# Reordering the steps of a compressed attention branch in a one-core decoder layer

## Chip, cores and metric

The kernel runs on one core of one Trainium2 chip. The metric is the device time of one execution in microseconds (us), as the median of three runs. The engines are named PE (TensorE, matrix multiply; PEld is its weight load), DVE (VectorE), ACT (ScalarE), POOL (GpSimd) and SP (SyncE, which here only issues the transfers).

## What is computed

One layer of a decoder on a sequence of 512 tokens with 1024 channels, in float32:

```python
h = rms_norm(x, attn_norm_w)
z = h @ w_in                      # pool input, q, k/v of three branches, gates
y_pool = pool_mixer(u_pool, pool_w, pool_scale) @ w_pool_br
y_attn = nsa_attention(q, k, v, nsa_g, ...) @ w_attn_br
x = x + (merge_g0 * y_pool + merge_g1 * y_attn) @ w_o
h = rms_norm(x, ffn_norm_w)
x = x + conv_ffn(h, w_up, conv_w, conv_b, w_down)
```

The attention has 16 heads of 64 channels in two groups of keys and values, and three branches whose outputs are added with sigmoid gates. Two of them see the 512 causal tokens (with 8 blocks out of 8 selected and a window of 512 both are plain causal attention, on keys and values of their own). The third one, the compressed branch, makes from the keys and from the values 31 blocks of 32 tokens each (stride 16), sends each block through a small network (`gelu(flat @ w1 + b1) @ w2`), and attends to those 31 keys.

## The kernel before

Every matrix product is done as three float32r products: each operand is split into a high part (a rounded copy, mostly on ACT, line 97) and a low part (the difference, on DVE or POOL, line 100), and `mm3` (lines 109 to 111) multiplies high by high, high by low and low by high. Weights come through a ring: `ring` (line 152) issues a transfer on SP into one of two `st` buffers and splits it into `hi` and `lo` tiles, of which there are six each. The kernel is written in a framework in which a program traces its instructions in order, and a scheduler then gives each engine a queue. It may move an instruction ahead of others on the same engine when those are not ready in its own estimate; on the chip every engine then works its queue in that order. Tiles of one tag in a pool share a fixed number of buffers. PSUM has eight banks: tag "g" (2 banks: `bank_g`), "s" (3, `bank_s`), "t" (2, `bank_t`) and "o" (1, `bank_o`).

The work before the attention stands as a list of calls (lines 529 to 553), and its order there is the priority that the scheduler sees:

- `kv_group(b)` and `q_group(gq)` (lines 338 and 357): a projection of 256 columns for four blocks of 128 tokens (`tg` in "s", 24 matmuls each), then norm and rope (`head_norm_rope`, line 285: on ACT x_, its square and a root; on DVE `hss`, two products and sum `h`, the reciprocal `hrs`, and `kd` or `qd`; a product on POOL), then transposes (`kt`, `qt` in "t") and the split into `KHL` or, for the queries, `qp` (lines 376 and 377, of tag "qo" with eight buffers).
- `pool_in`, `pool_mix`, `pool_out` (lines 392, 411, 424): the pooling mixer. `pool_mix` multiplies four groups (`pl` in "g") and splits them into `plo` (lines 102 and 103, tag "qo", too); `pool_out(c)` multiplies all four `plo` by a slice of `w_pbr` (`pb` in "g", two tiles, 24 matmuls).
- `cmp_in(i)` (line 440; i=0 keys, i=1 values): doubles the compressed branch's tokens on POOL (`dup`), transposes them (`ct`, two tiles in "t") and splits them into `X` (one buffer for both i), eight splits on ACT and DVE.
- `cmp_hid(i)` (line 459): two transfers of `cw1`, eight splits on ACT and POOL, 32 matmuls of 256 columns (`hp` in "g"), then `hs` (one instruction on ACT, two on DVE, lines 476 to 478), a transpose (`ht` in "g") and `cx`.
- `cmp_out(i)` (line 486): gelu by way of a tanh, the small product `kp` (in "o") and the split into `Kc` (keys) or `Vc` (values).
- `f_g0(c)` (line 525): a gate tile, 24 matmuls of 512 columns (`fm` in "g"), `zg` on DVE, tanh on ACT, `yp` on DVE.

The attention loop (lines 752 to 770) runs over 32 units u (head u // 2, branch u % 2) and one more turn. `scores(u)` (line 667) does for each block i of 128 queries the product `ss` in "s" (lines 691 and 692) and the softmax steps (lines 680 and 681); for i=0 both branches at once. `values(u)` (line 709) turns the probabilities (`tp`) and multiplies by the values (`op`). Between them lie `slot`s, at which PE gets pieces of gate tiles as filling (`fill`, line 590: `fm`, three matmuls a piece, kept behind the last `ss` by `issue_after`); the first two units get more of them (`START`, line 71: two pieces behind each `ss` of unit 0, one of unit 1). Weights for the filling are split ahead (`fetch`, line 579, the low part on POOL). The compressed branch is done for four heads at a time by `Cmp` (line 609): `score` (8 matmuls `sc`, then `cst` on DVE, line 624), `soft` (4 transposes `scq`, line 629, then the softmax, whose last step is `ce` on POOL, line 642) and `turn` (4 transposes `pct`, line 648, and `pc`), which `values` of the odd units reads (line 733). With `ORD = 0` and `DEPTH = 1` all three steps of the first four heads stand in turn u = 0: `score` and `soft` ahead of `scores(0)`, `turn` behind it.

Of the kernel before, what the change touches and what calls it, by code (L numbers as in the profile page):

```python
# [51 lines left out]
DEPTH = 1  # L52
# [6 lines left out]
ORD = 0  # L59
# [17 lines left out]
def layer(ctx: ExitStack, tc: tile.TileContext, par, masks, xT, w_kva, w_tm, w_fm, w_pl, w_pbr,  # L77
# [5 lines left out]
    def nm(s):  # L83
        cnt[0] += 1
        return f"{s}{cnt[0]}"
# [4 lines left out]
    def r32(ap):  # L90
        return ap.bitcast(F32)

    def split(hi, lo, src, scale=None, eng=None, cast=None):

        if scale is None:
            if cast is None:
                a.activation(hi, src, AF.Copy)  # L97
            else:
                cast.tensor_copy(hi, src)
            (eng or v).tensor_tensor(lo, src, r32(hi), ALU.subtract)  # L100
        else:
            a.activation(hi, src, AF.Copy, scale=scale)
            v.scalar_tensor_tensor(lo, src, scale, r32(hi), ALU.mult, ALU.subtract)
# [68 lines left out]
    def pv(n):  # L172
        o, w = _OFF[n]
        return pk[:, o:o + w] if o < NKEEP else pl_[:, o - NKEEP:o - NKEEP + w]
# [138 lines left out]
    def tok_gemm(ws, n):  # L313

        for t in range(NB):
            ps = bank_s("tg")
            tt = slice(t * P, (t + 1) * P)
            for k, (H, L) in enumerate(ws):
                pe.matmul(ps[:, :n], hh[k][:, tt], H, start=k == 0, stop=False)  # L319
                pe.matmul(ps[:, :n], hl[k][:, tt], H, start=False, stop=False)  # L320
                pe.matmul(ps[:, :n], hh[k][:, tt], L, start=False, stop=k == KC - 1)  # L321
            yield t, ps

    def tm_weights(i):
        return ring(w_tm[:, i, :1024], 256, 4, TW[i] and g) + ring(w_tm[:, i, 1024:], 256, 4, TW[i] and g)
# [12 lines left out]
    def kv_group(b):  # L338
        for t, ps in tok_gemm(tm_weights(b), 256):
            vin = heads(ps[:, 128:256])  # L340
            vh = V2[b][t][:, :, 0:DH]
            a.activation(vh, vin, AF.Copy, scale=rstd[:, t:t + 1])
            v.scalar_tensor_tensor(V2[b][t][:, :, DH:P], vin, rstd[:, t:t + 1], r32(vh), ALU.mult, ALU.subtract)

            k2 = pp.tile([P, 2, 2, DH], F32, tag="kq", name=nm("kd"), bufs=KQ)
            head_norm_rope(heads(ps[:, 0:128]), 2, t, 2 + b,
                           (k2, lambda x: x.unsqueeze(2).to_broadcast([P, 2, 2, DH])))
            tp = bank_t("kt")
            for G in range(2):
                pe.transpose(tp[:, G * P:(G + 1) * P], k2[:, G].rearrange("p a d -> p (a d)"), ident)  # L350
            tt = slice(t * P, (t + 1) * P)
            split(KHL[:, b, 0, :, tt], KHL[:, b, 1, :, tt], tp[:, :2 * P].rearrange("p (G q) -> p G q", q=P))
# [4 lines left out]
    def q_group(gq):  # L357
        qp = [qo.tile([P, 2, S], F32R, tag="qo", name=nm("qp"), bufs=8) for _ in range(2)]
        QP[2 * gq:2 * gq + 2] = qp
        for t, ps in tok_gemm(tm_weights(2 + gq), 256):  # L360


            q2 = pp.tile([P, 2, 2, DH], F32, tag="kq", name=nm("qd"), bufs=KQ)
            head_norm_rope(heads(ps[:, :256]), 4, t, 0,
                           (q2.rearrange("p b a d -> p a b d"),
                            lambda x: x.rearrange("p (a b) d -> p a b d", b=2)))
            if t % 2 == 0:
                tp = bank_t("qt").rearrange("p (b q) -> p b q", b=2)
            o = t % 2 * P
            for b in range(2):  # L370
                pe.transpose(tp[:, b, o:o + P], q2[:, b].rearrange("p a d -> p (a d)"), ident)
            if t % 2:
                tt = slice((t - 1) * P, (t + 1) * P)
                for a_ in range(2):
                    rh, rl = slice(64 * a_, 64 * a_ + 64), slice(64 - 64 * a_, 128 - 64 * a_)
                    a.activation(qp[a_][rh, :, tt], tp[rh], AF.Copy)
                    v.tensor_tensor(qp[a_][rl, :, tt], tp[rh], r32(qp[a_][rh, :, tt]), ALU.subtract)
# [46 lines left out]
    def pool_out(c):  # L424
        ws = ring(w_pbr[c], P, 8, POW[c] and g)
        for j in range(2):
            ps = bank_g("pb")
            mm3(ps, [(ws[2 * k + j], (plh[k], pll[k])) for k in range(4)])
            yp = ypp.tile([P, S], F32, tag=f"yp{2 * c + j}", name=f"yp{2 * c + j}")
            a.activation(yp, ps, AF.Copy, scale=0.5)  # L430
            ypool[2 * c + j] = yp
# [8 lines left out]
    def cmp_in(i):  # L440
        XX = p1.tile([P, 16, 2, 2, 32], F32R, tag="X", name=nm("X"))
        Xs[i] = XX
        X = (XX[:, :, 0], XX[:, :, 1])
        g.memset(r32(XX[:, :, :, 1, 31:32]), 0.0)
        split(X[0][:, :, 0, 31], X[1][:, :, 0, 31], pv("pos")[:, 16 * i:16 * i + 16])
        for G in range(2):
            tp = bank_t("ct")
            for t in range(NB):
                dup = p1.tile([P, 2, DH], F32, tag="dup", name=nm("dup"), bufs=3)
                g.tensor_copy(dup, kcd[i][t][:, G].unsqueeze(1).to_broadcast([P, 2, DH]))  # L450
                pe.transpose(tp[:, t * P:(t + 1) * P], dup.rearrange("p a d -> p (a d)"), ident)
            for lo_ in (0, 64):
                rr = slice(lo_, lo_ + 64)
                for c in range(2):

                    src = tp[rr].rearrange("p (n f b) -> p f n b", f=8, b=2)[:, :, c:c + 31, lo_ // 64]
                    split(X[0][rr, 8 * c:8 * c + 8, G, :31], X[1][rr, 8 * c:8 * c + 8, G, :31], src)

    def cmp_hid(i):
        X = Xs[i]  # L460
        hp = bank_g("hp")
        hv = hp[:, :256].rearrange("p (j h) -> p j h", j=2)
        for c in range(2):
            st = wr.tile([P, 1024], F32, tag="st", name=nm("st"), bufs=ring.bufs[0])
            nc.sync.dma_start(st, cw1[i, :, c * 1024:(c + 1) * 1024])
            for p_ in range(4):
                tag = ("hi", "lo")[p_ % 2]
                w = wr.tile([P, 2, 2, P], F32R, tag=tag, name=nm(tag), bufs=ring.bufs[1])
                split(w[:, 0], w[:, 1], st[:, 256 * p_:256 * p_ + 256].rearrange("p (b h) -> p b h", b=2),
                      eng=CW and g)  # L470
                for b in range(2):
                    q_ = 8 * c + 2 * p_ + b
                    pe.matmul(hv, X[:, q_].rearrange("p j g n -> p (j g n)"), w[:, :, b],
                              start=q_ == 0, stop=q_ == 15)
        hs = pp.tile([64, P], F32, tag="hs", name=nm("hs"))
        a.activation(hs, hp[:64, :P], AF.Copy)
        v.tensor_tensor(hs, hp[:64, P:256], hs, ALU.add)
        v.tensor_tensor(hs, hp[64:128, :P], hs, ALU.add)
        ht = bank_g("ht")
        pe.transpose(ht[:, :64], hs, ident[:64, :64])  # L480
        bias = pp.tile([P, 1], F32, tag="cb", name=nm("cb"))
        v.tensor_tensor(bias, ht[:, 31:32], b1[:, i:i + 1], ALU.add)
        cx[i] = pp.tile([P, 64], F32, name=f"cx{i}")
        v.tensor_scalar(cx[i], ht[:, :64], bias, None, ALU.add)
# [45 lines left out]
    for gi in range(4):  # L530
        pool_in(gi)
    kv_group(1)
    cmp_in(0)
    q_group(0)
    pool_mix()
    q_group(1)
    cmp_hid(0)
    cmp_in(1)
    pool_out(0)
    pool_out(1)  # L540
    q_group(2)
    pool_out(2)
    pool_out(3)
    cmp_hid(1)
    pre.close()
    q_group(3)
    mid = ExitStack()
    mp = pool(mid, "mp", side="right")
    for c in range(NPRE):
        f_g0(c, fm_tile(ring(w_fm[4 + c], P, KC), hh, hl), mp)  # L550
    cmp_out(0)
    cmp_out(1)
    mid.close()


# [193 lines left out]
    pcs = [Cmp(4 * q_) for q_ in range(4)]  # L749
    fetch(0)  # L750
    pbs = [None] * NU
    for u in range(NU + DEPTH):
        if u == ORD:
            pcs[0].score()
            pcs[0].soft()
        if u < NU:
            pbs[u] = scores(u)
        if u == max(ORD, DEPTH - 1):
            pcs[0].turn()
        w = u - DEPTH  # L760
        if w >= 0:
            values(w, pbs[w], pcs[w // 8])
            nq = w // 8 + 1
            if nq < 4:
                if w % 8 == 4:
                    pcs[nq].score()
                elif w % 8 == 5:
                    pcs[nq].soft()
                elif w % 8 == 7:
                    pcs[nq].turn()  # L770
# [195 lines left out]
```

## Time and profile before

| what | value |
|---|---|
| median of three runs | 843.49 us (843.36 to 844.0) |
| the profiled execution, its time | 842.97 us |
| its span, first to last instruction | 840.9 us |
| busy: PE, PEld | 817.7, 696.8 us |
| busy: DVE, ACT, POOL | 571.4, 464.4, 233.7 us |
| mean granted clock of PE | 0.994 |

All durations come from the one profiled execution. Times within it are us from the span's start. A busy PE means that matmuls are in flight. An engine's idle time matters only where it delays the end; here the chain that ended last goes through PE for 85% of the span. The granted clock is a share of full speed: 1.00 is 2.4 GHz, and 0.50 is the lower level of 1.2 GHz.

### The profile page before, as it was taken

Reading aid. Unit: us, or ns where it says so; the run is one execution under the profiler, and the core shown is the slowest. Engines: PE = TensorE matmul, PEld = TensorE weight load, DVE = VectorE, ACT = ScalarE, POOL = GpSimd, SP = SyncE. Lnnn points to the kernel's source line nnn. Section 1 sums busy time; section 2 is a strip of 40 time slices with the busy share of each in tenths; the row PEclk is TensorE's granted clock in tenths of the full one; section 3 lists DMA queues with packets and bytes.
Section 4 is the critical chain, followed back from the end, with each engine's and each line's share of the span. In section 5 each row is a group of like instructions: output and inputs, shape, how many; then the busy total and the mean of one; then the engine's idle time right before and its main releaser. Section 6 shows DMA issues by size and latency. Waiting matters only on the chain.

```text
span 840.9 us, 12107 instructions
## 1 busy us (share of the span) xinstructions
PE 817.7 (97%) x4291; PEld 696.8 (83%) x4291; DVE 571.4 (68%) x1194; ACT 464.4 (55%) x985; POOL 233.7 (28%) x326
## 2 busy tenths in 40 slices
PE   7999989989999999999999999999999999999998
PEld 6888878968878878788888888888888888888888
DVE  7599976778887888886565438877777777522321
ACT  6755767757787877785334436544554454322220
POOL 5696714347575655642001200000000000000000
PEclk9999989999999999999999999999999999999999
DMA  6333132330100101011443332233332333343430
GB/s 217 103 101 113 51 101 96 107 101 25 51 26 26 51 17 35 27 39 42 135 149 112 101 103 77 101 101 101 100 91 90 97 100 116 92 128 103 113 101 26
DMA packets 23116, 72.82 MB, mean 87 GB/s; under 512 B 2832, under 2 KB 3472, under 8 KB 23056
## 3 DMA queue, kind: packets, MB, share of 16 engines
q1 hardware_dynamic: 23056, 72.05, 27.5%
q8 instruction: 34, 0.56, 0.3%
q14 instruction: 26, 0.21, 0.1%
HBM read 69.94 MB, written 2.10 MB: 86 GB/s over the span
## 4 chain that ended last, share of the span: by engine, by line
PE 85%; DVE 7%; ACT 3%; DMA 2%; issue 1%; POOL 0%; SPq 0%; ACTq 0%; DVEq 0%; POOLq 0%
PE fm L109 16%; PE fm L111 16%; PE fm L110 16%; PE op L729 5%; PE dn L109 5%; PE dn L111 5%; PE dn L110 5%; PE tp L722 4%; PE ss L691 2%; PE ss L692 2%; PE tg L321 2%; PE tg L319 2%; PE tg L320 2%; DMA st<-in_w_fm 1%; PE pb L109 1%
## 5 line engine op out<-in xcount | busy, mean ns | idle before, releaser
L97 ACT ACTIVATE hi<-st 128x512 fp32r<-128x512 f32 (+3 forms) x253 | 152.2, 607 | 189.3 <-PE fm L110 89.6
L100 DVE TENSOR_TENSOR lo<-st,hi 128x512 fp32r<-128x512 f32 (+1 forms) x210 | 145.2, 695 | 100.5 <-ACT hi L97 99.2
L109 PE MATMUL fm<-h2h,hi 128*128 128x512 f32 x344 | 134.0, 389 | 0.0
L110 PE MATMUL fm<-h2l,hi 128*128 128x512 f32 x344 | 133.8, 389 | 0.0
L111 PE MATMUL fm<-h2h,lo 128*128 128x512 f32 x344 | 133.7, 389 | 0.0
L703 POOL TENSOR_TENSOR pb<-pb,sm 128x128 f32<-128x128 f32 (+3 forms) x128 | 91.8, 748 | 49.8 <-DVE sm L700 26.1
L681 ACT ACTIVATE pb<-pb,nm 128x384 f32<-128x384 f32 (+3 forms) x128 | 70.9, 555 | 16.2 <-DVE nm L680 15.4
L111 PEld LDWEIGHTS fm<-h2h,lo 128*128 128x128 f32 x344 | 64.6, 188 | 13.5
L110 PEld LDWEIGHTS fm<-h2l,hi 128*128 128x128 f32 x344 | 64.6, 188 | 13.4
L109 PEld LDWEIGHTS fm<-h2h,hi 128*128 128x128 f32 x344 | 64.6, 188 | 13.2
L109 PE MATMUL fm<-hh,hi 128*128 128x512 f32 x160 | 71.7, 448 | 0.0
L680 DVE CUSTOM_DVE_ANT_0 pb<-ss,mk 128x384 f32<-128x384 f32 (+3 forms) x128 | 58.9, 486 | 16.7 <-PE ss L692 13.2
L110 PE MATMUL dn<-gl,hi 128*128 128x512 f32 (+1 forms) x189 | 69.1, 365 | 0.0
L111 PE MATMUL dn<-gh,lo 128*128 128x512 f32 (+1 forms) x189 | 69.1, 365 | 0.0
L109 PE MATMUL dn<-gh,hi 128*128 128x512 f32 (+1 forms) x189 | 69.1, 365 | 0.0
L111 PE MATMUL fm<-hh,lo 128*128 128x512 f32 x160 | 63.4, 397 | 0.7 <-POOL lo L100 0.7
L100 DVE TENSOR_TENSOR ptl<-tp,pth 128x512 fp32r<-128x512 f32 (+1 forms) x96 | 56.6, 594 | 10.8 <-ACT pth L97 10.2
L110 PE MATMUL fm<-hl,hi 128*128 128x512 f32 x160 | 63.4, 396 | 0.0
L97 ACT ACTIVATE pth<-tp 128x512 fp32r<-128x512 f32 (+1 forms) x96 | 49.3, 517 | 22.8 <-PE tp L722 22.5
L100 POOL TENSOR_TENSOR lo<-st,hi 128x512 fp32r<-128x512 f32 x36 | 47.2, 1313 | 41.6 <-ACT hi L97 35.6
L319 PE MATMUL tg<-hi,hh 128*128 128x256 f32 x192 | 54.4, 286 | 0.0
L320 PE MATMUL tg<-hi,hl 128*128 128x256 f32 x192 | 54.4, 286 | 0.0
(256 smaller groups left out, 1815.9 us busy)
## 6 DMA issues: line engine op xcount, KB each, us to landing
st<-in_w_up SPq DMA_DIRECT2D x43, 512.0 KB, 3.5
st<-in_w_dn SPq DMA_DIRECT2D x24, 448.0 KB, 3.4
st<-in_w_fm SPq DMA_DIRECT2D x20, 512.0 KB, 3.5
st<-in_w_tm SPq DMA_DIRECT2D x12, 512.0 KB, 3.4
st<-in_w_ab SPq DMA_DIRECT2D x8, 512.0 KB, 3.5
st<-in_w_o SPq DMA_DIRECT2D x8, 512.0 KB, 3.4
x<-in_xT SPq DMA_DIRECT2D x15, 256.0 KB, 3.7
st<-in_cw SPq DMA_DIRECT2D x4, 512.0 KB, 3.5
```

The source lines that it names most:

```text
L97: a.activation(hi, src, AF.Copy)
L100: (eng or v).tensor_tensor(lo, src, r32(hi), ALU.subtract)
L109: pe.matmul(ps, sh, mh_, start=first and i == 0, stop=False)
L110: pe.matmul(ps, sh, ml_, start=False, stop=False)
L111: pe.matmul(ps, sl, mh_, start=False, stop=last and i == n - 1)
L319: pe.matmul(ps[:, :n], hh[k][:, tt], H, start=k == 0, stop=False)
L320: pe.matmul(ps[:, :n], hl[k][:, tt], H, start=False, stop=False)
L680: v.tensor_tensor_reduce(p_, ps, mcaus[:, S - n:], -1.0, 3e38, ALU.add, ALU.min, nm_[:, i:i + 1])
L681: a.activation(p_, p_, AF.Exp, bias=nm_[:, i:i + 1], scale=-1.0, accum_out=sm[:, i:i + 1])
L703: g.tensor_tensor(pb[:, PBASE[i]:PBASE[i] + n], pb[:, PBASE[i]:PBASE[i] + n], sm[:, i:i + 1].to_broadcast([P, n]), ALU.mult)
L722: last = pe.transpose(tp[:, n:n + P], pb[:, PBASE[i] + j * P:PBASE[i] + (j + 1) * P], ident)
L729: pe.matmul(op[:, j * P:], V2[b][j][:, G], pt_[:, TBASE[j]:TBASE[j] + w], start=b == 0 and j == 0 and part == 0, stop=False)
```

## The change

Two places change. In the list before the attention, `cmp_in(0)` goes behind `q_group(0)`, `pool_mix` behind `q_group(1)`, `cmp_hid(0)` behind `pool_out(0)`, `cmp_in(1)` behind `pool_out(1)`, `cmp_hid(1)` ahead of `pool_out(3)`, `cmp_out(0)` behind `q_group(2)`, and `cmp_out(1)` ahead of the two `f_g0`. In the attention loop `score` of the first four heads stays ahead of `scores(0)`, `soft` goes behind it, and `turn` goes behind `scores(1)`. No instruction is added or removed.

```diff
@@ -530,26 +530,26 @@
     for gi in range(4):
         pool_in(gi)
     kv_group(1)
+    q_group(0)
     cmp_in(0)
-    q_group(0)
+    q_group(1)
     pool_mix()
-    q_group(1)
+    pool_out(0)
     cmp_hid(0)
+    pool_out(1)
     cmp_in(1)
-    pool_out(0)
-    pool_out(1)
     q_group(2)
+    cmp_out(0)
     pool_out(2)
+    cmp_hid(1)
     pool_out(3)
-    cmp_hid(1)
     pre.close()
     q_group(3)
+    cmp_out(1)
     mid = ExitStack()
     mp = pool(mid, "mp", side="right")
     for c in range(NPRE):
         f_g0(c, fm_tile(ring(w_fm[4 + c], P, KC), hh, hl), mp)
-    cmp_out(0)
-    cmp_out(1)
     mid.close()
@@ -750,12 +750,13 @@
     fetch(0)
     pbs = [None] * NU
     for u in range(NU + DEPTH):
-        if u == ORD:
+        if u == 0:
             pcs[0].score()
-            pcs[0].soft()
         if u < NU:
             pbs[u] = scores(u)
-        if u == max(ORD, DEPTH - 1):
+        if u == 0:
+            pcs[0].soft()
+        if u == 1:
             pcs[0].turn()
```

## Rows read from the trace of the kernel before

**Rows 1.** The page: busy us (share of the span) and instructions.

```profile
PE 817.7 (97%) x4291; PEld 696.8 (83%) x4291; DVE 571.4 (68%) x1194; ACT 464.4 (55%) x985; POOL 233.7 (28%) x326
```

**Rows 2.** Waits of PE: us in total, times, longest us.

```profile
PE scq L629 <- DVE cst L624: 3.4, 1, 3.4
PE hp L473 <- DVE plo L103: 3.2, 1, 3.2
...
PE pl L109 <- DVE plo L103: 0.9, 2, 0.5
```

**Rows 3.** Stretches: us; PE, PEld, DVE, ACT, POOL busy (instructions); clock, DMA share, GB/s.

```profile
101.40:108.45 7.05, 2.59 (x12) 1.39 (x11) 6.83 (x14) 6.65 (x15) 3.50 (x5) 0.90 0.37 95
108.45:114.00 5.55, 5.55 (x26) 5.55 (x27) 5.36 (x11) 3.78 (x9) 0.15 (x1) 0.51 0.27 83
...
120.00:150.00 30.00, 30.00 (x169) 25.82 (x168) 18.91 (x46) 21.49 (x52) 11.16 (x18) 1.00 0.24 74
150.00:176.38 26.38, 26.38 (x177) 23.95 (x176) 20.89 (x45) 19.29 (x37) 10.52 (x13) 1.00 0.37 119
...
178.50:181.89 3.39, 0.00 (x1) 0.00 (x0) 2.69 (x7) 1.49 (x5) 1.26 (x1) 1.00 0.29 35
181.89:185.60 3.71, 3.71 (x13) 3.13 (x14) 2.37 (x8) 1.77 (x6) 0.00 (x0) 0.54 0.27 109
```

**Rows 4.** Timeline, 177 to 190 us: PE, DVE, POOL; last, one row of the chain.

```profile
181.89 0.90 PE L629 MATMUL scq<-pk,cst 128*128 128x128 f32 x4 [3.39 <-DVE cst L624]
...
180.10 0.69 DVE L527 SCALAR_TENSOR_TENSOR yp<-zg,yp 128x512 f32<-128x512 f32 x1 [0.57 <-ACT zg L522]
...
181.15 0.69 DVE L624 TENSOR_TENSOR cst<-sc,mk 128x512 f32<-128x512 f32 x1
...
178.64 1.26 POOL L100 TENSOR_TENSOR lo<-st,hi 128x512 fp32r<-128x512 f32 x1 [1.33 <-ACT hi L97]
...
189.61 1.05 POOL L642 TENSOR_TENSOR ce<-ce,csm 128x512 f32<-128x512 f32 x1 [0.38 <-DVE csm L640]
...
185.99 0.23 PE fm L109
```

**Rows 5.** Timeline, 82 to 103 us: the second pl on PE, then ACT.

```profile
82.08 0.39 PE L111 MATMUL pl<-pli,plw 128*128 128x512 f32 x1
...
100.26 0.59 ACT L376 ACTIVATE qp<-qt 64x512 fp32r<-64x512 f32 x1
100.88 1.27 ACT L102 ACTIVATE plo<-pl,pk 128x512 fp32r<-128x512 f32 x2
```

**Rows 6.** Stretch 84 to 110.11: all; tile h; tile X; tile qp; group hrs.

```profile
84.00:110.11 26.11, 21.65 (x166) 20.29 (x164) 24.77 (x57) 20.21 (x50) 17.39 (x30) 0.94 0.26 82
...
84.00:110.11 26.11, 12.69 (x28) 5.28 (x12) 7.87 (x14) 0.94 0.26 82
...
84.00:110.11 26.11, 1.66 (x8) 1.66 (x8) 3.30 (x8) 2.94 (x8) 0.00 (x0) 0.94 0.26 82
...
84.00:110.11 26.11, 0.00 (x0) 0.00 (x0) 2.06 (x4) 2.35 (x4) 0.94 0.26 82
...
L305 DVE RECIPROCAL hrs<-hss 128x4 f32<-128x4 f32 x7 | 1.2, 168 | 0.0
```

**Rows 7.** Timeline around hp and ht: PE at 118.68 and 151.97, DVE at 154.69.

```profile
118.68 0.27 PE L480 MATMUL ht<-pk,hs 64*128 64x64 f32 x1
...
151.97 0.28 PE L319 MATMUL tg<-hi,hh 128*128 128x256 f32 x1
...
154.69 0.29 DVE L478 TENSOR_TENSOR hs<-hp,hs 64x128 f32<-64x128 f32 x1
```

**Rows 8.** Timeline: kp of cmp_out(0) on PE, the table load on ACT, cw on SP.

```profile
124.76 0.28 PE L109 MATMUL kp<-hd,w2d 128*128 128x64 f32 x1
...
118.97 1.28 ACT L492 ACT_TABLE_LOAD   x1
...
80.66 10.20 SPq L465 DMA_DIRECT2D st<-in_cw  x2
```

## Prediction

> **What bounds the kernel now.** I read the busy shares first [rows 1]: TensorE (PE) is busy for 817.7 of 840.9 us, VectorE (DVE) for 571.4, ScalarE for 464.4. So only time in which PE is idle, or runs at a lower clock, can be won: 23.2 us of idle time in all. The list of PE's waits comes second [rows 2]. Its two longest entries are single stalls, 3.4 us in front of scq (the transposes of Cmp.soft, waiting for cst on DVE) and 3.2 us in front of hp (the matmuls of cmp_hid, waiting for plo on DVE). Both lie where the diff acts. The third view, busy time by stretch [rows 3], shows what each costs. From 101.4 to 108.45 us PE works for 2.59 of 7.05 us, and from 108.45 to 114.0 the granted clock is 0.51, so about half of 5.55 us is lost again: 4.46 + 5.55 x 0.49 = 7.2 us for stall A. From 178.5 to 181.89 PE does nothing, then 3.71 us pass at 0.54: 3.39 + 3.71 x 0.46 = 5.1 us for stall B. Between the two, from 120 to 176.38, PE has no idle time at all. Whatever the change does has to be read at these two places, and in whether the full stretch between them stays full.
>
> **Stall B, the first turns.** PE runs its matmuls in the order of its queue. After the eight sc matmuls the next entry is scq, and scq needs cst, which DVE runs at 181.15, behind zg and yp of the last f_g0 tile (yp stands at 180.10, behind ScalarE's tanh) [rows 4]. The first head's scores (ss) need only queries and keys that are long finished, yet they stand behind scq. In the changed order unit 0's scores come between: four pairs of ss, and behind each pair six fill matmuls of 512 columns (the START slots), 0.23 us each in the chain [rows 4]. The pairs have 256, 256, 384 and 512 columns, twice, at that pace 1.26 us. That is 24 x 0.23 + 1.26 = 6.8 us of work, more than the 3.39 us that is now empty. The weights for these fills are ready: the last of GpSimd's four lo tiles of that stretch starts at 178.64 and takes 1.26 us [rows 4]. So the 5.1 us can go. What is late next: the banks of tag "s" are three, and the third score pair (i=2) needs the bank of sc, free when cst has run at 181.15 + 0.69 = 181.84. PE asks for it at 178.5 + 12 x 0.23 + 2 x 0.23 = 181.7. That is a tie, and any lateness of DVE becomes a stall. I charge 0.6 us (one 128x512 DVE instruction more in front of cst), with 0 and 2 us as ends. Gain at B: 4.5 us (3.1 to 5.1).
>
> soft now has its DVE steps during unit 1's scores, and turn stands behind them. From scq at 181.89 to the start of the last step of soft, ce on GpSimd, 7.7 us pass [rows 4]; unit 1's scores (nine fills and three pairs, 3.1 us) cover a part of that. The rest lies beside the pb transposes of the first values step and the scores of unit 2, which need nothing from it: pc is read only at the end of unit 1's values (L733). So soft and turn cost nothing as long as PE's queue has such work ahead of pct; if it has not, 7.7 - 3.1 = 4.6 us is the upper end.
>
> **Stall A, the order of the steps before.** Tiles of one tag are handed out in the order in which the program asks for them. The trace shows it: the first plo stands on ScalarE directly behind the second qp of q_group(0), though its own pl matmul was done at 82.5 [rows 5]. So pool_mix was held by q_group(0), and that by cmp_in(0): the transposes ct hold both "t" banks until the X splits are through. In the new order q_group(0) gets its banks first. But plo is now handed out behind qp of q_group(1), and pool_out(0) is the first to wait for plo in the place of cmp_hid(0).
>
> DVE sets this time. From 84 to 110.11, the end of the last plo, it is busy for 24.77 of 26.11 us [rows 6]: there is no gap to speak of, and 1.054 us of wall time per busy us. Before pb can start in the new order DVE must do nearly the same set. One rope set is less (four tokens' blocks of q_group(0) and two of q_group(1) have to be done, where seven are now: 12.69 / 7 + 0.17 = 2.0 us). Three qp are more (six for three: 2.06 us). Of the eight X splits (3.30 us) at least four are needed. That is 23.2 to 24.8 us busy, 24.5 to 26.2 us of wall time: pb could start at 108.5 to 110.2, where hp started at 108.45. If the scheduler also puts the last two rope sets of q_group(1) in front, as the program order now says, 4.0 x 1.054 = 4.2 us come on top: 114.4. PE's own work up to there is unchanged, so its idle time shifts by the same amount. I take the middle of the pair, 109.35: a loss of 0.9 us (ends 0 and 5.95). The low clock behind the stall stays.
>
> At this place the page "Perfetto Trace Analysis" of the Trainium skill (section Optimization Strategy) warns that a gap which repeats on the engine that should be full can mean that there isn't room for the next tile. By that rule stall A would come back in front of the next user of the bank, at its full price, and once more at each later user. The rows show single gaps, not a repeating one; what the rule would make of the time is the first rival below.
>
> **The small chain of cmp_hid.** hp, hs, ht: hs is one ScalarE and two DVE instructions, and ht needs the other "g" bank. For i=1 hp ends by 151.97 + 0.16 and the last hs at 154.69 + 0.29, 2.85 us; for i=0 ht came only at 118.68 [rows 7]. Now it costs nothing, since tg matmuls of q_group fill PE from 151.97 on. In the new order the next user of the "g" banks is pool_out, which asks behind ht and must wait; and the tg weights come behind pool_out's in the ring of six hi/lo tiles, so this cover is partly gone. Left over are the transposes ct and qt and a late tg. Ends: 0, and 2 x 2.85 = 5.7 us. The nearest waits that the trace does show, pl behind a small DVE step in the same "g" banks, are two of 0.45 us on average [rows 2], so I take 0.45 for each: 0.9 us.
>
> **Steps at no cost.** cmp_out(0) is written last, but its kp matmuls already run at 124.76 [rows 8], since the scheduler fills gaps; its new place changes little. cmp_out(1) moves ahead of f_g0, with a tanh table load on ScalarE (1.28 us [rows 8]) hidden by PE's f_g0 matmuls; its four Vc splits leave DVE's queue ahead of cst, worth a little at B. The DMAs keep their number and sizes. In the queue on SP the first w_pbr now goes ahead of the two cw [rows 8], which start at 80.66; hp isn't wanted before 108, so the cover is tens of us. GpSimd's splits for cw and its dup copies move with their steps; GpSimd is busy for 17.39 us of the 26.11 above [rows 6], so it isn't late.
>
> **The sum.** -4.5 + 0.9 + 0.9 = -2.7 us. The profiled execution took 842.97 us, its span is 840.9; the median of the three runs is 0.52 above it. 842.97 - 2.7 = 840.3, as a median 843.49 - 2.7 = **840.8 us**. About 0.2% (1.7 us) is what a measurement of this kernel can tell from no change.
>
> **The rivals.** *Stall A grows (slower).* DVE does all of q_group(1)'s rope before plo, pb starts at 114.4, and one of the two hs chains stands bare: +5.95 + 2.85, against -4.5 at B: +4.3, 847.8 us. It decides from the point where A and the chains together cost 4.5 + 1.7 = 6.2 us. For it: DVE has no gap from 84 on, and the program order does put pool_mix last. Against: the scheduler deals by readiness, as kp shows. This is also what the page's rule gives. Chance 0.28. *Given back (same).* cst comes late because q_group(3)'s qp is later at the same time, so only 3.1 us are won at B, and A and the chains take +1.5 and +1.2: -0.4, 843.1 us. That covers a scheduler which ends up with nearly the old order, too. Chance 0.25. *Both stalls go.* If q_group(0), no longer behind cmp_in(0) for its banks, lets plo run ahead of X, PE never runs dry: -7.2 - 4.5 + 0.9 = -10.8, 832.7 us. For it: q_group(0)'s qp do wait for those banks now [rows 5]. Against: DVE's sum. Chance 0.10.
>
> **How the numbers follow.** The forecast has 0.37; with the large gain, faster is 0.47, same 0.25, slower 0.28. The forecast's own range is 838.5 to 843 us. Left out are most of the large gain (0.08) and the top of the slower case (0.10): 836.8 to 847.5.
>
> **What would show it.** Right at B: no scq wait of 3.4 us in PE's list, ss directly behind sc, clock 1.0 from 178 to 186. Wrong at B: PE waiting in ss for cst, or in pct for ce. At A: pb, not hp, is first behind the gap, between 108 and 110.5; a start after 112 makes the slower rival right. A wait of PE in ht or in the pb behind it of more than 1 us shows the hs chain bare. The prediction is wrong if the stretch between the stalls, full now, shows over 3 us of idle time.

## The result and the profile after

The changed kernel takes 849.56 us (848.53 to 850.68, four runs) beside 843.42 us (843.24 to 844.0) of the kernel before: a ratio of 1.0072 (95% interval 1.0054 to 1.0089), slower by 6.1 us. The forecast was 840.8 us. The profiled execution took 850.4 us, its span is 848.4.

The page and PE's list of waits of the changed kernel, beside [rows 1, 2]:

```profile
PE 821.5 (97%) x4291; PEld 698.7 (82%) x4291; DVE 571.8 (67%) x1194; ACT 462.4 (55%) x985; POOL 231.0 (27%) x326
```

```profile
PE qt L371 <- DVE X L100: 3.6, 2, 3.4
PE qt L371 <- DVE qd L311: 2.4, 3, 1.0
PE pct L648 <- POOL ce L642: 2.0, 1, 2.0
...
PE ct L451 <- POOL dup L450: 1.9, 1, 1.9
```

The scq stall of 3.4 us and the hp stall of 3.2 us are gone. In their places stand pct, which waits for the last step of soft, and, where hp waited for plo, the transposes qt and ct, which wait for X, for qd and for the copies dup. The stretches, with the columns of [rows 3]:

```profile
101.40:108.45 7.05, 1.74 (x13) 1.34 (x13) 6.07 (x16) 5.80 (x19) 6.85 (x12) 0.94 0.27 74
108.45:114.00 5.55, 4.06 (x14) 2.50 (x15) 4.64 (x9) 3.29 (x6) 1.96 (x6) 0.50 0.29 94
114.00:120.00 6.00, 6.00 (x22) 4.54 (x21) 2.46 (x4) 1.97 (x3) 0.59 (x2) 0.68 0.00 0
120.00:150.00 30.00, 30.00 (x195) 27.15 (x195) 19.34 (x49) 20.20 (x50) 9.92 (x17) 1.00 0.27 89
150.00:176.38 26.38, 24.14 (x158) 21.54 (x158) 20.78 (x44) 18.68 (x38) 7.78 (x11) 1.00 0.39 114
...
183.68:192.32 8.64, 8.64 (x41) 7.16 (x40) 4.75 (x15) 4.82 (x13) 2.67 (x3) 1.00 0.27 83
...
200.00:207.40 7.40, 5.42 (x21) 4.05 (x21) 3.08 (x5) 3.06 (x7) 7.10 (x10) 0.56 0.00 0
...
60.98:183.68 122.70, 111.92 (x741) 100.73 (x740) 98.33 (x216) 79.25 (x188) 55.08 (x92) 0.96 0.30 92
```

The last row's counterpart in the kernel before:

```profile
60.03:176.38 116.35, 110.09 (x742) 100.63 (x740) 95.66 (x211) 79.72 (x184) 56.69 (x92) 0.97 0.31 95
```

PE still runs dry from 101.4 on, and the low clock now lasts from 108.45 to 120. Behind sc (183.68) PE is full at full clock, which is what the change wanted there, but from 200 to 207.4 it idles for 2 us and runs at 0.56.

As a mark ahead of everything that the diff touches serves kt, here and in the texts of the experiments: the group of four kt matmuls that starts at 60.03 before and at 60.98 after (there called the first kt, though two others stand 8 us ahead of it). sc is the border between the list and the attention. From kt to sc pass 176.38 - 60.03 = 116.35 us before and 122.70 after; from sc to the end of the span 840.9 - 176.38 = 664.5 and 848.4 - 183.68 = 664.7. So the list costs 6.35 us and the loop wins nothing. Of the 6.35, 4.5 are idle time of PE (122.70 - 111.92 = 10.8 us, where the same reading of before gives 116.35 - 110.09 = 6.3): 2.3 between 101.4 and 120 (6.8 against 4.5) and 2.2 between 150 and 176.38, where before had none. The rest is PE's longer busy time for the same matmuls, at a mean clock of 0.96 instead of 0.97. The other 0.9 us of this execution lie ahead of the diff, and a second set of the changed kernel doesn't have them all (below).

The timeline of the changed kernel around the first place and, in its last five rows, around pct:

```profile
104.56 0.33 PE L451 MATMUL ct<-pk,dup 128*128 128x128 f32 x1 [1.88 <-POOL dup L450]
108.33 1.08 PE L371 MATMUL qt<-pk,qd 128*128 128x128 f32 x4 [3.43 <-DVE X L100]
...
100.18 0.59 DVE L311 TENSOR_TENSOR qd<-h,hrs 128x256 f32<-128x256 f32 x1
...
116.45 0.79 PE L109 MATMUL pb<-plo,hi 128*128 128x512 f32 x1
...
110.79 0.59 ACT L376 ACTIVATE qp<-qt 64x512 fp32r<-64x512 f32 x1 [0.75 <-DVE qp L377]
111.40 1.27 ACT L102 ACTIVATE plo<-pl,pk 128x512 fp32r<-128x512 f32 x2
...
202.55 1.12 PE L648 MATMUL pct<-pk,ce 128*128 128x128 f32 x4 [1.98 <-POOL ce L642]
203.46 1.06 PE L722 MATMUL tp<-pk,pb 128*128 128x128 f32 x4
...
199.58 0.23 DVE L640 TENSOR_SCALAR csm<-csm,pk 128x4 f32<-128x4 f32 x1
...
199.74 1.75 POOL L703 TENSOR_TENSOR pb<-pb,sm 128x128 f32<-128x128 f32 x3 [1.90 <-DVE sm L700]
201.45 1.04 POOL L642 TENSOR_TENSOR ce<-ce,csm 128x512 f32<-128x512 f32 x1
```

Its plo stands directly behind a qp of q_group(1), 10.5 us later than in [rows 5], and pb, first in need of it, starts at 116.45. The row of qd is the second of the two that this first qt of q_group(1) needs: it was done at 100.77, 7.6 us ahead of qt.

### The profile page after: what moved, and what is told of

Its sections match the earlier page's. It is cut to its first block, busy times and chain, and to the rows that moved or that the text cites. A ratio compares the mean times of both kernels' runs of the same rounds, so it can differ in the third digit from the quotient of the medians.

```text
span 848.4 us, 12107 instructions
## 1 busy us (share of the span) xinstructions
PE 821.5 (97%) x4291; PEld 698.7 (82%) x4291; DVE 571.8 (67%) x1194; ACT 462.4 (55%) x985; POOL 231.0 (27%) x326
## 4 chain that ended last, share of the span: by engine, by line
PE 83%; DVE 8%; DMA 3%; ACT 3%; issue 2%; POOL 1%; SPq 0%; ACTq 0%; DVEq 0%
PE fm L111 16%; PE fm L109 16%; PE fm L110 16%; PE op L729 5%; PE dn L109 5%; PE dn L110 5%; PE dn L111 5%; PE tp L722 4%; PE ss L692 2%; PE ss L691 2%; DMA st<-in_w_tm 1%; PE tg L321 1%; PE tg L319 1%; PE tg L320 1%; DVE lo L100 1%
```

## The experiments

Sixteen sets ran, each beside runs of the kernel before on the same chip (medians 843.45 to 843.74 us). All but the second set of the changed kernel are edits of one or of both places; e2_again repeats e2_list. Two theories go through them: Q, that pct's place in PE's queue is what the loop costs, and T, that plo, held back behind q_group(1), is what the list costs. The rival to T is that other work (DVE's, GpSimd's) sets the time there anyway. The two readings, kt to sc and sc to the end of the span, are worked out as above from each profiled execution (us):

| kernel | edit, in words | median | ratio (95%) | kt to sc | sc to end |
|---|---|---|---|---|---|
| before | | 843.42 | 1 | 116.35 | 664.5 |
| after | both places | 849.56 | 1.0054 to 1.0089 | 122.70 | 664.7 |
| r_after | the same, again | 850.03 | 1.0065 to 1.0091 | 122.89 | 665.3 |
| e1_loop | the loop alone | 843.15 | 0.9990 to 1.0007 | 116.28 | 664.4 |
| e2_list | the list alone | 845.84 | 1.0019 to 1.0044 | 122.91 | 663.5 |
| e2_again | the same, again | 845.86 | 1.0021 to 1.0045 | 123.04 | 660.3 |
| e3_turn | loop alone, turn behind values(0) | 840.16 | 0.9950 to 0.9974 | 116.29 | 661.1 |
| e8_list_turn | changed list, e3's loop | 845.96 | 1.0017 to 1.0040 | 122.99 | 660.5 |
| e4_mix | before, pool_mix first | 843.78 | 0.9999 to 1.0015 | 117.19 | 664.3 |
| e12_mix_late | before, pool_mix behind q_group(1) | 847.78 | 1.0034 to 1.0058 | 119.80 | 665.8 |
| e5_cmpin | changed list, cmp_in(0) put back | 845.60 | 1.0014 to 1.0032 | 119.87 | 662.9 |
| e6_mixq1 | changed list, pool_mix put back | 840.41 | 0.9951 to 0.9976 | 117.31 | 659.7 |
| e13_tiles | after, plo's tiles asked for early | 850.99 | 1.0068 to 1.0098 | 122.90 | 665.5 |
| e15_owntag | after, two plo in a tag of their own | 849.48 | 1.0057 to 1.0082 | 122.43 | 663.6 |
| e9_combo | e6's list, e3's loop | 840.39 | 0.9950 to 0.9974 | 117.37 | 660.4 |
| e7_early_out | plo and pb early, e3's loop | 839.36 | 0.9936 to 0.9963 | 115.01 | 661.7 |
| e14_best | e7, cmp_out early | 839.94 | 0.9945 to 0.9970 | 115.72 | 662.6 |
| e10_cmp_first | pool_mix, then cmp_in(0), first | 841.06 | 0.9954 to 0.9980 | 118.11 | 660.6 |

The columns separate cleanly: one list gives nearly one value from kt to sc, whatever the loop (116.3 for the list of before, 122.7 to 123.0 for the changed one).

### The two places apart

**e1_loop** has the list of before and the changed loop.

```diff
-        if u == ORD:
+        if u == 0:
             pcs[0].score()
-            pcs[0].soft()
...
-        if u == max(ORD, DEPTH - 1):
+        if u == 0:
+            pcs[0].soft()
+        if u == 1:
             pcs[0].turn()
```

> The loop's part alone (soft behind scores(0), turn behind scores(1)), on the old list. Theory Q (queue place): pct stands in PE's queue ahead of the first tp, and ce is late since soft's DVE steps now share DVE with the softmax of units 1 to 3; that stall takes what the scq stall gave back, so 843.4 us within 1.5, with no scq wait and a pct wait on ce of 1.5 to 3 us. Rival I (the two parts of the change disturb each other, and the loop alone is sound): -4.5 us, 839 us, no pct wait.

It took 843.15 us, no different from before (ratio 0.9998). In PE's list of its waits scq is gone and pct has come:

```profile
PE pct L648 <- POOL ce L642: 2.3, 1, 2.3
...
PE ss L691 <- DVE nm L680: 1.1, 2, 0.5
```

The stretch behind it is half empty, at a lower clock:

```profile
192.00:200.00 8.00, 5.16 (x21) 3.49 (x22) 4.66 (x14) 4.33 (x11) 6.48 (x10) 0.82 0.00 0
```

So the loop's gain is given back inside the loop, as Q says.

**e2_list** and **e2_again** have the changed list, which begins as here, and the loop of before; **r_after** is the changed kernel again.

```diff
     kv_group(1)
+    q_group(0)
     cmp_in(0)
-    q_group(0)
+    q_group(1)
     pool_mix()
-    q_group(1)
+    pool_out(0)
     cmp_hid(0)
...
```

> The list's part alone, on the old loop. Theory Q: all of the loss is here, +6 to +7 us, 849.5 us, with the scq wait of about 3.4 us still there and the waits of qt on X and of ct on dup as in the changed kernel. Rival I: the loop part won 4.5 us and the list lost 10.6, so 854 us.

> The changed list with the old loop, a second time. If the list's loss is the same under every loop (+5.8 under the loop with the late turn, +6.9 under the changed loop), the time is 848.5 to 850 us, as in the profiled execution of the first time, 849.33. If the old loop takes a part of the loss back, as the first median said, it is 845 to 846.5 us, and the scq wait is shorter than the 3.4 us of before, or the stretch behind it fuller.

> The changed kernel again, beside the others on one chip. Theory S (sum of parts: the list alone cost 2.6 us, the loop alone nothing): 845.8 to 846.5 us, and the first measurement of 849.6 had a few more low-clock stretches. Rival P (the parts make each other worse: the list delays the softmax of the first units, so the pct wait and the low clock behind it grow): 849 us or more again.

r_after repeats the loss (850.03 us, plo on ScalarE at 110.74). The time is what P forecast, and P's mechanism is there in a small part: pct waits for 2.29 us in r_after and in e1_loop alike, but the low clock lasts longer (a mean of 0.89 over the 30 us from sc on, 0.94 in e1_loop), and sc to the end takes 0.9 us more. The rest comes from what the list does under the loop of before. The list alone has a median of 845.85 us in both sets, below both expectations of e2_list, while single runs reach 849. Its two profiled executions show both outcomes; from kt to sc they take the same time (122.91 and 123.04 us). The one that took 849.33 us, stretch and timeline:

```profile
189.25:194.75 5.50, 5.50 (x22) 4.68 (x23) 3.00 (x10) 2.30 (x8) 0.00 (x0) 0.69 0.22 80
```

```profile
189.25 0.70 PE L629 MATMUL scq<-pk,cst 128*128 128x128 f32 x4 [3.32 <-DVE cst L624]
...
172.28 1.78 DVE L100 TENSOR_TENSOR lo<-st,hi 128x512 fp32r<-128x512 f32 x1
...
172.07 3.14 POOL L100 TENSOR_TENSOR lo<-st,hi 128x512 fp32r<-128x512 f32 x2 [1.11 <-PE tg L321]
```

The one that took 846.06 us, the same:

```profile
187.49:193.00 5.51, 5.51 (x29) 4.74 (x30) 4.30 (x13) 3.25 (x10) 1.04 (x1) 1.00 0.20 79
```

```profile
187.49 0.66 PE L629 MATMUL scq<-pk,cst 128*128 128x128 f32 x4 [1.55 <-DVE cst L624]
...
171.61 0.68 DVE L100 TENSOR_TENSOR lo<-st,hi 128x512 fp32r<-128x512 f32 x1
...
171.72 3.14 POOL L100 TENSOR_TENSOR lo<-st,hi 128x512 fp32r<-128x512 f32 x2 [1.26 <-PE tg L320]
```

There scq waits for 1.55 us and the clock stays at 1.00; in the other it waits for 3.32 and 5.5 us at 0.69 follow. From sc to the end these are 660.3 and 663.5 us. The difference of 1.77 us in front of scq starts long before sc, in the rows of lo shown. Where DVE's lo starts ahead of GpSimd's splits it takes 0.68 us, where it starts behind them 1.78. These 1.1 us, and 0.6 that DVE was late already (counted from kt), stay in DVE's rows up to cst. Whether the same instruction parts the single runs, no trace shows.

So under the loop of before the changed list often takes back a part of stall B: cst starts 2.8 us behind sc in the quicker execution, 4.6 in the other, 4.8 in the kernel before. In the changed loop this is worth nothing, because scq no longer stands directly behind sc. That is why the list (845.85 - 843.6 = +2.3) and the loop (0) alone don't add up to +6.1.

### The loop: where turn stands

**e3_turn** leaves the list of before. soft is behind scores(0), as in the change, but turn is behind values(0). **e8_list_turn** is the same loop on the changed list.

```diff
-        if u == 1:
-            pcs[0].turn()
...
             values(w, pbs[w], pcs[w // 8])
+            if w == 0:
+                pcs[0].turn()
```

> The loop's part on the old list, with turn one step further back, behind values(0). Theory Q: pct no longer stands in front of tp and op of unit 0, so the gain of the scq stall is kept: -4.5 us, 839 us, no pct wait over 0.5 us. Rival D (DVE and POOL are simply full there, whatever PE's order): tp waits for the scaled pb in the place of pct, at most -1.5 us, 842 us or more.

> The new list with the loop whose turn stands behind values(0). Theory Q (the place of pct in the queue is the whole of what the loop lost): 3 to 3.5 us below the new list alone and 4 or more below the changed kernel, 842.5 us. Rival D (behind the new list DVE and POOL are so late that tp or op waits instead): 845 us or more, with tp or op waits over 1.5 us near 200 us.

e3_turn is quicker than before by 3.6 us (843.71 in its set), e8_list_turn than the changed kernel in the same set by 4.1. The wait in pct is gone from PE's list, and in e3_turn's stretches the clock holds:

```profile
184.00:192.00 8.00, 8.00 (x43) 6.41 (x41) 6.86 (x23) 6.39 (x17) 5.54 (x6) 1.00 0.23 67
192.00:200.00 8.00, 7.79 (x48) 6.84 (x47) 6.82 (x27) 7.37 (x24) 6.10 (x10) 1.00 0.00 2
200.00:207.40 7.40, 6.39 (x35) 4.80 (x34) 5.83 (x14) 4.93 (x13) 5.77 (x8) 1.00 0.05 17
```

One step later in the order, the same four transposes cost nothing. Against the changed loop, Q holds on both lists. Against the list alone it doesn't: e8_list_turn wins nothing (845.96 beside 845.85 us), where Q forecast 3 to 3.5 us, since the list alone had mostly lost its stall B already (sc to the end 660.3 in its quicker execution, 660.5 here). Its time lies in the range of D, but the waits that D names aren't there: op waits twice for 0.9 us in all, tp for 0.2.

### The list: what holds plo

**e4_mix** moves pool_mix ahead of cmp_in(0) in the kernel before, **e12_mix_late** only behind q_group(1).

```diff
+    pool_mix()
     cmp_in(0)
     q_group(0)
-    pool_mix()
     q_group(1)
```

```diff
     q_group(0)
-    pool_mix()
     q_group(1)
+    pool_mix()
     cmp_hid(0)
```

> The old kernel with pool_mix moved ahead of cmp_in(0) and q_group(0), and nothing else. Theory T (tags are handed out in program order, and plo hangs on qp of q_group(0)): plo runs soon after pl, before 92 us, both g banks are free when hp is due, and stall A shrinks from 7.2 us to under 2: 837 to 839 us. Rival V (VectorE's total work sets the time): X and the rest are as late as before, hp starts at 107 or later, 842 to 844 us.

> The kernel before with one edit: pool_mix behind q_group(1). If plo's place in the order of its tag is what costs the changed list its time, plo stands behind the qp of q_group(1) on ScalarE, at 108 us or later, hp can't start before 113, and the time is 847 to 850 us. If the move of cmp_in(0) behind q_group(0) is what costs it, this kernel is within 2 us of before: 841.5 to 845.5 us.

e4_mix has its first plo at 79.40, and hp starts at 104.82 instead of 108.45, yet the time is that of before: PE waits for 2.8 us in qt for X, the next in line. So plo early is what T says it is, but alone it wins nothing, as the rival has it; the price of T, 837 to 839 us, was wrong. e12_mix_late loses 4.3 us by one moved line. Its plo on ScalarE:

```profile
110.23 0.59 ACT L376 ACTIVATE qp<-qt 64x512 fp32r<-64x512 f32 x1 [1.11 <-DVE qp L377]
110.85 1.26 ACT L102 ACTIVATE plo<-pl,pk 128x512 fp32r<-128x512 f32 x2
```

That is the picture of the changed kernel, with hp at 115.90, and without any wait for dup. So pool_mix's place is enough for a part of the loss.

**e6_mixq1** and **e5_cmpin** are the changed list with one step put back, pool_mix ahead of q_group(1) or cmp_in(0) ahead of q_group(0), on the loop of before.

```diff
     cmp_in(0)
+    pool_mix()
     q_group(1)
-    pool_mix()
     pool_out(0)
```

```diff
+    cmp_in(0)
     q_group(0)
-    cmp_in(0)
     q_group(1)
```

> The new list with one call put back: pool_mix ahead of q_group(1) as it was; the old loop. Theory T (plo hangs on the qp that is asked for just before it; with q_group(1) in front it waits for the t banks that ct and the X splits hold): plo at about 101 us, the first pb near 106 instead of 116, 842 to 843.5 us, at least 2.5 below the new list alone. Rival X (the hole is q_group(1) itself waiting for X, and no PE work fits in): within 1 us of the new list alone, 845 to 846.5.

> The changed list with cmp_in(0) back ahead of q_group(0), on the old loop. If plo's place behind q_group(1) is the whole cost, sc stays 119.5 to 122.5 us behind the first kt, as in the kernel with pool_mix alone moved (119.8) or the changed list (122.9), and the time is 844 to 848 us. If cmp_in(0), behind q_group(0) and with its copies late on POOL, is a cause of its own, sc comes under 118 us behind the first kt and the time is under 842 us.

With pool_mix put back, the list turns from a loss into a gain of 3.3 us:

```profile
90.88 0.59 ACT L376 ACTIVATE qp<-qt 64x512 fp32r<-64x512 f32 x1
91.49 1.27 ACT L102 ACTIVATE plo<-pl,pk 128x512 fp32r<-128x512 f32 x2
...
102.96 0.40 PE L109 MATMUL pb<-plo,hi 128*128 128x512 f32 x1
...
113.54 1.09 PE L371 MATMUL qt<-pk,qd 128*128 128x128 f32 x4 [3.52 <-DVE qp L377]
```

pb fills the hole from 102.96 to 108.94, and a hole of 3.5 us opens in front of the next qt. So up to sc this list still takes 1.0 us more than that of before (117.31 against 116.35); its gain lies behind sc, where scq waits for only 1.2 us. With e12_mix_late and e5_cmpin this makes a square of the two moves, from kt to sc: neither 116.35, cmp_in(0) alone 117.3 (e6_mixq1), pool_mix alone 119.8 (e12_mix_late and e5_cmpin), both 122.7. The sum of the single prices is 1.0 + 3.45 = 4.4 us, and the pair costs 6.35. So e5_cmpin's 119.87 doesn't say that plo's place is the whole cost: putting cmp_in(0) back wins 3.0 us of the changed list's 122.9. The other moves of the list are worth nothing that can be seen there (e12_mix_late and e5_cmpin differ in them, and agree).

**e13_tiles** and **e15_owntag** ask how plo is held. The first asks for the four tiles ahead of q_group(1) and leaves pool_mix where the change put it; the second takes two of the four from a tag of their own.

```diff
     cmp_in(0)
+    mix_tiles()
     q_group(1)
     pool_mix()
```

```diff
-            pt_ = qo.tile([P, 2, S], F32R, tag="qo", name=nm("plo"), bufs=8)
+            pt_ = (p1.tile([P, 2, S], F32R, tag="plo", name=nm("plo"), bufs=2) if gi < 2
+                   else qo.tile([P, 2, S], F32R, tag="qo", name=nm("plo"), bufs=8))
```

> The changed kernel with one edit: the four plo tiles are asked for ahead of q_group(1), while pool_mix itself, its instructions and its weights, stays behind q_group(1). If the order in which tiles of one tag are handed out is what holds plo, ScalarE has its first plo before 105 us, sc starts some 6 us earlier relative to the start of the work (117 to 118.5 us behind the first kt, where the changed kernel has 122.8), and the time is 843 to 846 us, the loop's lost 4 us still in it. If it is the place in the list, by which the scheduler puts the rope steps of q_group(1) ahead of plo on DVE and ScalarE, plo stays at 110 us or later and the time at 848.5 to 850.5 us.

> The changed kernel with one edit: the first two plo tiles come from a tag of their own, the last two stay in qo. If a buffer of a tag is handed out in the order of the first writes in the list, the first two plo stand on ScalarE before 95 us, ahead of the qp of q_group(0), while the last two, in the same program and of the same step, stay behind the first qp of q_group(1), at 108 us or later; pb still needs all four, so the time comes down by 1 to 3 us only, to 847 to 849 us. If it is pool_mix's place in the list and not the buffers, all four stay at 110 us or later, and the time is 849.5 to 851 us.

Asking early changes nothing: in e13_tiles plo stays at 111.17. In e15_owntag the two kinds part, within one program and one step:

```profile
83.66 0.68 ACT L102 ACTIVATE plo<-pl,pk 128x512 fp32r<-128x512 f32 x1
84.54 0.69 ACT L102 ACTIVATE plo<-pl,pk 128x512 fp32r<-128x512 f32 x1
...
110.75 0.59 ACT L376 ACTIVATE qp<-qt 64x512 fp32r<-64x512 f32 x1 [0.49 <-DVE qp L377]
111.36 1.27 ACT L102 ACTIVATE plo<-pl,pk 128x512 fp32r<-128x512 f32 x2
...
101.48 0.39 PE L109 MATMUL pl<-pli,plw 128*128 128x512 f32 x1
...
107.70 0.47 PE L452 MATMUL ct<-pk,dup 128*128 128x128 f32 x1 [4.33 <-POOL dup L451]
...
113.50 0.79 PE L109 MATMUL pb<-plo,hi 128*128 128x512 f32 x1
```

The two of their own tag are done at 85, the two of "qo" stand behind a qp of q_group(1), although their pl matmuls started at 101.48. So, as far as these two runs show, a buffer is handed out in the order in which the steps stand that first write to the tag's tiles. The time, though, can't be told from that of the changed kernel (849.48 beside 849.56 and 850.03 us), where 1 to 3 us less were expected: pb starts 3 us sooner, but PE now waits for 4.33 us in ct for a dup copy, and sc stands only 0.3 us nearer to kt. The late copies on GpSimd are the second hold; with cmp_in(0) back ahead of q_group(0) (e5_cmpin) no wait for them is left.

### Versions that beat both

**e9_combo** joins the list of e6_mixq1 and the loop of e3_turn. **e7_early_out** (list of before) and **e10_cmp_first** (changed list) put pool_mix right behind kv_group(1), with e3's loop, the second with cmp_in(0) next. **e14_best** moves cmp_out forward in e7_early_out. The start of e7's list against that of before:

```diff
     kv_group(1)
-    cmp_in(0)
-    q_group(0)
     pool_mix()
+    q_group(0)
+    pool_out(0)
+    cmp_in(0)
     q_group(1)
...
```

In e10_cmp_first the same place, against the list of before, too, and in e14_best the end of e7's list:

```diff
     kv_group(1)
+    pool_mix()
     cmp_in(0)
     q_group(0)
-    pool_mix()
+    pool_out(0)
     q_group(1)
...
```

```diff
     q_group(2)
+    cmp_out(0)
...
     q_group(3)
+    cmp_out(1)
...
-    cmp_out(0)
-    cmp_out(1)
```

> The changed list with pool_mix back ahead of q_group(1) (worth -3.3 us alone on the old loop), together with the loop in which turn stands behind values(0) (worth -3.5 us alone on the old list). If the two places are independent the gains add: about 837 us. Rival: on this list the scq wait in the old loop was only 1.2 us, so the loop has less left to win there and the sum comes to 839.5 us. Either way no wait in scq or pct over 1 us, and sc at about 177.7.

> A version meant to be the best: the loop with turn behind values(0), and a list with pool_mix ahead of q_group(0) and pool_out(0) ahead of cmp_in(0) and q_group(1), so that PE has pb matmuls, which ask little of DVE, where it now runs dry. Theory F (stall A is a lack of PE work that doesn't need DVE): 836 to 838 us, less than 3 us of idle time between 100 and 114. Rival V (DVE's total work sets when hp and q_group(2) can go; pb only moves the hole): 840 us as with the loop alone.

> pool_mix first, then cmp_in(0) ahead of q_group(0), pool_out(0) right behind q_group(0) and pool_out(1) behind q_group(1) and cmp_hid(0), with the turn behind values(0). If what counts is that plo is handed out early, so that pb can stand wherever the t banks are held up, PE has pb matmuls for the hole and the time is 836 to 838 us. Rival: cmp_in(0) in front holds the t banks for its X splits as in the kernel before, q_group(0) and (1) are pushed back, and the hole opens in front of qt: 840 us or more.

> The quickest list so far (pool_mix first, then q_group(0), pool_out(0), cmp_in(0), q_group(1)), with the turn behind values(0), and with cmp_out(1) ahead of the two f_g0 as in the changed kernel. In the kernels that have cmp_out early, 660.4 to 660.6 us pass from sc to the end with this turn, in those that have it late 661.1 to 661.7. If that is cst coming sooner, the time is 838 to 838.6 us; if it is chance, 839.4 us as in the kernel without the edit.

e7_early_out is the quickest, 839.36 us, 4.4 below before. e9_combo shows that the two gains are one: 840.39 us, as with either part alone. On e6's list the scq wait was already down to 1.2 us at full clock, so e3's loop found nothing left to win. e10_cmp_first, at 841.06 us, went the rival's way. e14_best is no better than e7_early_out, so the early cmp_out is worth nothing there; cst even comes later, and ss waits for it for 1.5 us, where it waits for 0.4 in e7_early_out. In none of them is the hole of the first place gone. e7_early_out was expected at 836 to 838 us with less than 3 us of idle time between 100 and 114; it has 4.1, since qt waits for 4.3 us from 109.9 on. Why this hole stays when plo is early is open: DVE is busy there for 12.4 of 14 us, so that its total work sets the time, as the rival to T says, isn't excluded.

## Why the prediction was wrong

The sum had -4.5 us behind sc and +1.8 ahead of it. Measured were +0.2 and +6.35, so a step failed at each place.

**Stall B, the stall itself: right.** The scq wait went, ss stands directly behind sc, and the clock is 1.00 from 183.68 to 192.32. The 0.6 us charged for the bank of sc were not needed in the changed kernel.

**Soft and turn: the step that failed first.** They were to "cost nothing as long as PE's queue has such work ahead of pct", with 4.6 us as the upper end; 0 was taken. The work was there, but on the wrong side: the scheduler put the ss of units 2 and 3 ahead of pct, and tp of the first values step behind it. Those ss waited twice for 0.5 us, pct for 2.0, and 5.42 us of matmuls ran at 0.56: 1.1 + 2.0 + 5.42 x 0.44 = 5.5 us, as much as the 5.1 of stall B. ce was later, too: from scq to the start of ce on GpSimd pass 192.32 to 201.45, 9.1 us instead of 7.7. That isn't DVE, as the expectation of e1_loop had it: csm, the last step of soft on DVE, is done at 199.81, 7.5 us behind scq, as early as before (7.6). GpSimd's queue has three products pb ahead of ce, from 199.74 on, and ce starts when they are through. No run takes them out of its way. e1_loop shows the loss without the list. e3_turn, whose ce is just as late (9.1 us behind scq), removes it by pct's place alone.

**"DVE sets this time": the step that failed at stall A.** pb was put at 109.35 (at worst 114.4) and came at 116.45. The step took DVE's sum for the path and left out the wait for a bank. plo has to wait for qp of q_group(1) by the order of its tag; that qp waits for qt, qt for the "t" banks that ct holds, those for X, and X for the dup copies. The qd for this qt were done at 100.77, and qt starts at 108.33. The prediction stated the tag's order, and even that plo is now handed out behind qp of q_group(1), but then counted only DVE's work up to there. Stretch 84 to 110.11 of the changed kernel, all and tile h, beside [rows 6]:

```profile
84.00:110.11 26.11, 20.61 (x165) 19.58 (x164) 24.12 (x61) 17.97 (x49) 15.53 (x31) 0.95 0.22 69
...
84.00:110.11 26.11, 14.51 (x33) 5.97 (x14) 7.06 (x15) 0.95 0.22 69
```

DVE was hardly less busy than before (24.12 us, 24.77 before), but with other work. While qt waited, it took what was ready, the rope of all four blocks of q_group(1) but the last qd, as in the slower rival: 14.51 us of h, where the sum took 12.69 - 2.0 = 10.7. plo hadn't begun. So it wasn't the sum of DVE's work that plo waited for. What part DVE's full queue has in X being late (its X splits stand among the rope, from 102.66 to 109.45) no run separates. By e12_mix_late, in which no engine has an instruction more, 3.45 us come with pool_mix's place alone. Measured at sc: +6.35 us where 0.9 + 0.9 were charged.

On the same point the wording was a little off. Tiles are handed out not as the program asks for them (e13_tiles), but in the order of the steps that first write them (e15_owntag).

The warning of the Trainium skill's "Perfetto Trace Analysis" (section Optimization Strategy), that a gap which repeats can mean that there is no room for the next tile, was nearer to it. The trace agrees in part: plo got no buffer of its tag, and qt waited for 3.4 us for a bank. But it is not one gap that repeats; the waits beside it, 1.9 us in ct and 1.0 in qt, are for a copy and for qd. That the gap returns "at its full price" is what the prediction made of the page.

**The small chain of cmp_hid: right in size.** ht waits for 0.8 us; 0.9 was charged for both chains. The stretch that was full before, though, has 2.2 us of idle time from 150 to 176.38:

```profile
152.04 0.44 PE L371 MATMUL qt<-pk,qd 128*128 128x128 f32 x2 [0.94 <-DVE qd L311]
...
153.25 0.24 PE L480 MATMUL ht<-pk,hs 64*128 64x64 f32 x1 [0.77 <-DVE hs L478]
```

The rest of it is qt waiting for qd, here and once more for 0.4 us at 168.56, which no term had.

**"GpSimd is busy for 17.39 us of the 26.11, so it isn't late": wrong.** From 101.4 to 108.45 GpSimd is busy for 6.85 of 7.05 us. The splits for cw stand between the dup copies, and ct waits 1.9 us for one of them (4.3 in e15_owntag). A mean over 26 us can't show that.

**cmp_out(1) ahead of f_g0, "worth a little at B": not shown.** In the list alone scq waits for 1.55 us in one execution and 3.32 in the other, and the 1.1 us shown above don't come from cmp_out(1). In e14_best its early place brought no gain, and in the changed loop nothing is left for it to win.

**The rivals.** "Stall A grows" named what happened at A, and that pb would start after 112. Its 847.8 us was too low because it kept the 4.5 us at B; its own prices (5.95 + 2.85) were above the 6.35 measured. That both mechanisms would go wrong together was in no case, and so the range ended at 847.5.

## What to carry to other kernels

Before a step is moved, list the shared pools that it writes to (buffers of a tag, banks), and which step's first write now stands ahead of it: as plo here, it may not start sooner than that one, however early its inputs are there. When work is to hide a wait, ask on which side of the waiting instruction it stands in the queue of the engine; work that the scheduler has put behind it, or already used up ahead of it, hides nothing. And gains at one stall don't add: a list and a loop that each take away the same wait are worth it once.

## What was not expected of the hardware

One DVE instruction, the low part lo of a weight (128x512, two operands in SBUF), takes 0.68 us when it starts 0.11 us ahead of GpSimd's splits, and 1.78 us when it starts 0.21 us behind them (the two executions of the list alone shown above; the changed kernel has 1.78 us, too, at 172.07). The Trainium skill's "SBUF — State Buffer" (section SBUF: two separate sides) says that such a DVE instruction and a GpSimd instruction that reads SBUF exclude each other on a shared pair of ports, and that the one that starts first has it for its whole instruction. The trace agrees, with 1.1 us for one instruction.

PE's gap of 1.55 us left the granted clock at 1.00, where the one of 3.32 us at the same place, in the same program, was followed by 5.5 us at a mean of 0.69, between its two levels of 1.2 and 2.4 GHz. With 1.77 us less of waiting, the time from sc to the end was 3.3 us shorter. So a gap that is halved can win more than its half.
